# Differential attention scores: from twelve half-row matmuls a head to eight full-row ones

## The chip, the cores and the metric

The kernel runs on one core of one Trainium2 chip. The metric is the time of one execution on the device, in microseconds (us). A core has engines that run side by side, each with its own queue: TensorE multiplies matrices (PE in the profile, its weight loads are PEld), VectorE (DVE) and ScalarE (ACT) work element by element, GpSimd (POOL) does almost nothing here, and SyncE (SP) issues the transfers of the weights. An engine starts its instructions in the order of its queue; between engines there are semaphores.

A matmul takes a stationary operand (rows of the contraction by 128 columns), which a weight load puts into the array, and streams a moving operand through it. Its rows are the partitions of the on-chip memory: a contraction of 128 uses all 128 rows, one of 64 uses rows 0 to 63 or rows 64 to 127.

## The reference, cut to what matters

Two layers of an encoder with 256 tokens and 2048 features. In each layer a differential attention with 8 heads stands beside a latent attention with 8 heads; both are gated, summed and projected, and a feed-forward part and a gated embedding part follow. The part that the change touches:

```python
dq = apply_partial_rope(dq.reshape(b, s, 2 * DIFF_HEADS, DIFF_HEAD_DIM), cos_p, sin_p)
dk = apply_partial_rope(dk.reshape(b, s, 2 * DIFF_HEADS, DIFF_HEAD_DIM), cos_p, sin_p)
...
scores = jnp.einsum('bqhcd,bkhcd->bhcqk', qb, kh).astype(jnp.float32) * scale
probs = jax.nn.softmax(scores, axis=-1)
weights = probs[:, :, 0] - lam * probs[:, :, 1]
```

So each head has two attention maps (c = 0 and 1), each with its own 64 features of query and key, its own 256 x 256 scores and its own softmax; the second map is subtracted with a learned factor. All data are 32-bit floats.

## The kernel before, in words

**Numbers in two parts.** TensorE multiplies a shortened 32-bit format (float32r in the code). The kernel keeps precision by splitting each operand into two parts: the leading bits (hi), which ScalarE makes by a copy that rounds, and the rest (lo), which VectorE makes by subtracting hi from the number. A product a*b is then hi*hi + hi*lo + lo*hi. The function `split` (line 254) does this for activations, into a tile of 512 columns: hi of the 256 tokens, then their rest. The function `piece` (176) does it for weights: SyncE loads up to 128 x 1024 numbers, ScalarE writes `whi`, VectorE writes `wlo` (line 194; the subtraction is recorded at line 76, in the helper `tt`). `whi` and `wlo` have three buffers each. `emit` (216) issues, for each 128 x 128 block, one matmul of 512 columns with the hi weights (219) and one of 256 columns with the lo weights (223). `joined` (247) adds the two halves of the result: a ScalarE copy and a VectorE addition.

**The stage.** Activations are kept transposed: features on the partitions, tokens along the row. Within a layer, the differential heads come first. For a head h, `queries_keys(h)` (551) multiplies the layer's input with the query weights and then with the key weights of the head, 16 blocks each. Rows 0 to 63 of the result are map 0, rows 64 to 127 are map 1. Each result is joined, rotated (a shuffle of rows, two multiplications by the tables `sr` and `cr`, and an addition, all on VectorE) and split: the query into `ub[h]`, the key into the buffer `fa(h)`.

`diff_weights(h)` (662) computes the two score maps. The three products of the parts are listed by `three` (410), and `scores` (413) issues them for each block of 128 queries, the two maps in turn, so that a matmul on rows 64 to 127 and one on rows 0 to 63 alternate (line 421):

```python
def three(q, k):
    return [(q[:, :T], k[:, T:]), (q[:, T:], k[:, :T]), (q[:, :T], k[:, :T])]
```

That is 2 maps x 2 blocks x 3 products = 12 matmuls of 64 rows a head. `exps` (424) does the softmax of one map: the maximum of each row (VectorE, 427), a scaling of it, two exponentials with row sums (ScalarE, 430), a reciprocal (VectorE, 431). Then the two maps are combined into one matrix of weights E (669, 670), `turned` (434) transposes it on TensorE through `ident` (439) into a buffer with the tag `wt`, and `diff_out` (673) multiplies it with the values (679). Its result goes into `fa(h)`, by then free of the keys.

The latent attention's heads, later, use `scores` too, but with all 128 rows: ten matmuls of 256 columns a head. Its rotated queries are stored in another form, by the last branch of `rotated` (387 to 391): one ScalarE copy of 512 columns writes the rounded number twice, and two subtractions of 64 rows overwrite half of each copy with the rest, so that 128 rows hold the leading bits of 64 features and their rest.

**Order.** The loop `pipelined` (697) interleaves: it computes the scores of head h + 1 while the output of head h is made, and between these steps it takes one step of `beside` (604), which holds the products of later heads, the latent keys and queries, and the first gates. The program is written in that order, and a planner then orders the instructions of all engines by a timeline of its own: an instruction that can't start gives way to a later one that can. That is why scores of a head may stand in the middle of a later product. Buffers of one tag are handed on when their last reader is done; the planner inserts these waits.

Of the kernel before, what the change touches and what calls it, by code (L numbers as in the profile page):

```python
# [24 lines left out]
DH = 8  # L25
# [29 lines left out]
def encoder(ctx, tc, x, p, positions, cols, lams, wq, wk, wv, wcq, wckv, wkr, wga, wgb,  # L55
            w_q_up, w_kn, w_v, w_bd, w_bm, w_out, w_gate, w_up, w_down, w_pin, w_pg, rope_c, out):
    nc = tc.nc
    V, A, PE = nc.vector, nc.scalar, nc.tensor
# [4 lines left out]
    tmp = pool("tmp")  # L63
    stat = pool("stat")
# [4 lines left out]
    def scratch(tag, bufs, n=T):  # L69
        return tmp.tile([P, n], F32, tag=tag, name=tag, bufs=bufs)  # L70
# [4 lines left out]
    def tt(o, a, b, op):  # L75
        return V.tensor_tensor(out=o, in0=a, in1=b, op=op)  # L76

    def stt(o, a, s, b, op0, op1):
        return V.scalar_tensor_tensor(out=o, in0=a, scalar=s, in1=b, op0=op0, op1=op1)
# [40 lines left out]
    halves = rc[:, 4 : 4 + P]  # L120
# [28 lines left out]
    neg_lam = const.tile([P, DEPTH], F32, name="neg_lam")  # L149
# [97 lines left out]
    def joined(acc, o=None):  # L247
        t = scratch("join", 3)
        A.activation(t, acc[:, T:], AF.Copy)  # L249
        o = scratch("a", 4) if o is None else o  # L250
        tt(o, acc[:, :T], t, ALU.add)
        return o

    def split(u, src, gain=None):
        hi, lo = u[:, :T], u[:, T:]
        if gain is None:
            return A.activation(hi, src, AF.Copy), tt(lo, src, hi.bitcast(F32), ALU.subtract)  # L257
        return A.activation(hi, src, AF.Copy, scale=gain), stt(lo, src, gain, hi.bitcast(F32), ALU.mult, ALU.subtract)
# [108 lines left out]
    for t in krs:  # L367
        nc.gpsimd.memset(t.bitcast(F32), 0.0)

    def rotated(a, c_, s_, o=None):  # L370
        if o is None:
            r = bank()[:, :T]
            PE.matmul(r, halves, a, start=True, stop=True)
        else:
            r = a
        t = scratch("sh", 2)
        V.stream_shuffle(t, r, SWAP16)
        tt(t, t, s_, ALU.mult)
        tt(a, r, c_, ALU.mult)
        tt(a, a, t, ALU.add)  # L380
        if o is None:
            hi, rest = krs
            A.activation(hi[:, :T], a, AF.Copy)
            for j in range(2):
                s, t = slice(64 * j, 64 * j + 64), slice(j * T, (j + 1) * T)
                tt(rest[s, t], a[s], hi[s, :T].bitcast(F32), ALU.subtract)
        else:
            A.activation(o.rearrange("p (h t) -> p h t", h=2), a.rearrange("p (h t) -> p h t", h=1).to_broadcast([P, 2, T]), AF.Copy)
            for j in range(2):
                s, t = slice(64 * j, 64 * j + 64), slice(j * T, (j + 1) * T)  # L390
                tt(o[64 - 64 * j : 128 - 64 * j, t], a[s], o[s, t].bitcast(F32), ALU.subtract)

    def narrow(src, us):

# [15 lines left out]
    def three(q, k):  # L410
        return [(q[:, :T], k[:, T:]), (q[:, T:], k[:, :T]), (q[:, :T], k[:, :T])]

    def scores(*maps):


        Ss = [bank(ps_s, "S", "S", (P, 2, T)) for _ in maps]
        for b in range(2):
            for j in range(len(maps[0])):
                for S, pairs in reversed(list(zip(Ss, maps))):
                    q, k = pairs[j]  # L420
                    PE.matmul(S[:, b, :], q[:, b * P : (b + 1) * P], k, start=j == 0, stop=j == len(pairs) - 1)  # L421
        return Ss

    def exps(S, E, scale):

        nm, sm, rs = (stat.tile([P, 2], F32, tag=t, name=t, bufs=4) for t in ("nm", "sm", "rsum"))
        V.tensor_reduce(out=nm, in_=S, axis=AX.X, op=ALU.max, negate=True)
        ts(nm, nm, scale, None, ALU.mult)
        for b in range(2):
            last_exp[0] = A.activation(E[:, b, :], S[:, b, :], AF.Exp, bias=nm[:, b : b + 1], scale=scale, accum_out=sm[:, b : b + 1])  # L430
        V.reciprocal(out=rs, in_=sm)
        return rs
# [72 lines left out]
    for L in range(DEPTH):  # L505
# [38 lines left out]
        cr, sr, crm, srm = (t[:, j, :] for t in (fc(0), fc(1)) for j in range(2))  # L544
# [1 line left out]
            tt(o, t, R, ALU.mult)  # L546


        qk = [(ub[h], operand(fa(h, F32R))) for h in range(DH)]

        def queries_keys(h, *inside):
            for which, w in enumerate((wq, wk)):
                a = joined(product(w[L, h], ua, inside=(8, inside[which]) if inside else None))
                sh = scratch("sh", 2)
                V.stream_shuffle(sh, a, ROPE16)
                tt(sh, sh, sr, ALU.mult)
                tt(a, a, cr, ALU.mult)
                tt(a, a, sh, ALU.add)
                split(qk[h][which], a)


        cq, ckv = ub[8:12], ub[12:14]
# [99 lines left out]
        def diff_weights(h):  # L662
            q, k = qk[h]
            E = [weights(), weights("E1")]
            halves = [slice(c * 64, (c + 1) * 64) for c in range(2)]
            r = [exps(S, e, 0.125) for S, e in zip(scores(*(three(q[d], k[d]) for d in halves)), E)]
            ts(r[1], r[1], neg_lam[:, L : L + 1], None, ALU.mult)
            for b in range(2):
                A.activation(E[0][:, b, :], E[0][:, b, :], AF.Copy, scale=r[0][:, b : b + 1])
                stt(E[0][:, b, :], E[1][:, b, :], r[1][:, b : b + 1], E[0][:, b, :], ALU.mult, ALU.add)  # L670
            return E[0]

        def diff_out(h, W):
# [97 lines left out]
        for part, (f0, f1) in enumerate(FF_PARTS):  # L771
            for f in range(f0, f1):
                a = pre.pop(0) if pre else joined(product(w_gate[L, f], ub))
                tt(a, a, R, ALU.mult)
                s = scratch("sig", 2)
# [3 lines left out]
                b = pre.pop(0) if pre else joined(product(w_up[L, f], ub))  # L779
# [241 lines left out]
```

## Time and profile before

The profile is one execution, read by the hardware profiler.

| What | Value |
|---|---|
| time, median of 3 runs | 2827.17 us (2827.13 to 2827.33) |
| time of the profiled execution | 2827.12 us |
| its span, first to last instruction | 2825.3 us |
| TensorE busy | 2816.8 us, 100% |
| TensorE weight loads busy | 2490.3 us, 88% |
| VectorE busy | 2080.3 us, 74% |
| ScalarE busy | 1534.1 us, 54% |
| mean granted TensorE clock | 0.999 |
| bytes moved by DMA | 531.37 MB, mean 188 GB/s |

A row of a timeline gives the start, the duration, the engine, the line in the kernel, the instruction, what it writes and reads by the program's names, and the shapes (partitions x elements). Instructions on an engine overlap: the next one starts before the last one has ended. What an instruction costs in a full queue is therefore the distance from its start to the next start. In a row with "x12", twelve instructions of one kind are merged, and the duration reaches from the first start to the last end. The differential heads of the first layer lie at about 100 to 220 us of the span, those of the second at about 1504 to 1624 us.

### The profile page before, as it was taken

What the parts mean: (1) busy time and instruction counts of PE and PEld (TensorE: products, weight loads), DVE (VectorE), ACT (ScalarE), POOL (GpSimd) and SP (SyncE); (2) the same over time, 40 slices, a digit from 0 to 9 for tenths busy, and PEclk for the clock granted to TensorE, in tenths of its full rate; (3) what the DMA queues carried; (4) which work ended last, traced back from release to release, by engine and by line L of the source; (5) the groups of instructions that cost most, each with busy time, mean ns of one, the idle gap of its engine ahead of it and who ended that gap; (6) DMA issues with size and microseconds to landing.
All of it is one profiled execution on the core that took longest, in us unless ns stands there. A gap on an engine that the chain in (4) does not pass through costs nothing.

```text
span 2825.3 us, 43994 instructions
## 1 busy us (share of the span) xinstructions
PE 2816.8 (100%) x16691; PEld 2490.3 (88%) x16691; DVE 2080.3 (74%) x3573; ACT 1534.1 (54%) x2556; POOL 1.9 (0%) x15
## 2 busy tenths in 40 slices
PE   9999999999999999999999999999999999999998
PEld 8888988888888888888888889888888888888888
DVE  8998668776666666677869976687766666666777
ACT  7676546554444444455646765465544444444556
POOL 0000000000000000000000000000000000000000
PEclk9999999999999999999999999999999999999999
DMA  7545456555665566666665454555566655655654
GB/s 246 174 162 172 157 186 197 193 193 194 188 198 194 190 194 198 193 194 193 194 193 166 157 173 157 193 198 193 194 194 189 198 193 185 202 194 194 193 193 155
DMA packets 158325, 531.37 MB, mean 188 GB/s; under 512 B 17184, under 2 KB 25376, under 8 KB 158112
## 3 DMA queue, kind: packets, MB, share of 16 engines
q1 hardware_dynamic: 157680, 527.96, 58.2%
q8 instruction: 131, 2.15, 0.3%
q14 instruction: 82, 0.67, 0.1%
q10 hardware_dynamic: 432, 0.59, 0.1%
HBM read 526.39 MB, written 2.10 MB: 187 GB/s over the span
## 4 chain that ended last, share of the span: by engine, by line
PE 99%; DMA 0%; DVE 0%; SPq 0%; DVEq 0%; ACT 0%; issue 0%
PE mm L219 61%; PE mm L223 31%; PE S L421 1%; PE mmv L481 1%; PE mmv L483 1%; PE mmv L482 1%; PE at L439 1%; PE at L679 1%; PE at L735 0%; PE mm L826 0%; PE mm L407 0%; DMA w<-in_wv 0%; PE at L694 0%; PE at L332 0%; PE mm L882 0%; PE at L300 0%
## 5 line engine op out<-in xcount | busy, mean ns | idle before, releaser
L194 ACT ACTIVATE whi<-w 128x1024 fp32r<-128x1024 f32 (+2 forms) x1038 | 1065.9, 1028 | 1224.9 <-issue 593.4
L76 DVE TENSOR_TENSOR wlo<-w,whi 128x1024 fp32r<-128x1024 f32 (+2 forms) x1038 | 1225.8, 1182 | 648.0 <-ACT whi L194 642.3
L219 PE MATMUL mm<-ub,whi 128*128 128x512 f32 x3936 | 1340.5, 389 | 0.0
L219 PE MATMUL mm<-ua,whi 128*128 128x512 f32 x3712 | 1274.0, 390 | 0.0
L223 PE MATMUL mm<-ub,wlo 128*128 128x256 f32 x3936 | 1084.6, 276 | 0.0
L223 PE MATMUL mm<-ua,wlo 128*128 128x256 f32 x3712 | 1027.4, 277 | 0.0
L219 PEld LDWEIGHTS mm<-ub,whi 128*128 128x128 f32 x3936 | 737.8, 188 | 151.8
L219 PEld LDWEIGHTS mm<-ua,whi 128*128 128x128 f32 x3712 | 696.2, 188 | 141.5
L223 PEld LDWEIGHTS mm<-ub,wlo 128*128 128x128 f32 x3936 | 738.8, 188 | 1.3
L223 PEld LDWEIGHTS mm<-ua,wlo 128*128 128x128 f32 x3712 | 697.1, 188 | 2.0
L76 DVE TENSOR_TENSOR a<-mm,join 128x256 f32<-128x256 f32 (+1 forms) x423 | 174.8, 417 | 1.7 <-ACT join L855 1.4
L249 ACT ACTIVATE join<-mm 128x256 f32<-128x256 f32 x452 | 165.6, 368 | 6.3 <-PE mm L223 5.7
L76 DVE TENSOR_TENSOR xT<-xT,mm 128x256 f32<-128x256 f32 x256 | 106.9, 420 | 40.8 <-PE mm L223 37.0
L76 DVE TENSOR_TENSOR a<-a,row 128x256 f32<-128x256 f32 (+1 forms) x209 | 87.6, 422 | 5.9
L76 DVE TENSOR_TENSOR a<-a 128x256 f32<-128x256 f32 x120 | 50.9, 425 | 4.0
L76 DVE TENSOR_TENSOR ua<-a,ua 128x256 fp32r<-128x256 f32 x120 | 50.0, 418 | 1.0 <-ACT ua L257 1.0
L257 ACT ACTIVATE ua<-a 128x256 fp32r<-128x256 f32 x120 | 48.1, 403 | 2.6 <-DVE a L76 2.6
L481 PE MATMUL mmv<-whi,ua 128*128 128x512 f32 x128 | 49.0, 394 | 0.4 <-ACT whi L194 0.2
L430 ACT ACTIVATE E<-S,nm 128x256 f32<-128x256 f32 x96 | 44.2, 472 | 8.0 <-DVE nm L82 8.0
L482 PE MATMUL mmv<-whi,ua 128*128 128x512 f32 x128 | 48.4, 391 | 0.0
L483 PE MATMUL mmv<-wlo,ua 128*128 128x512 f32 x128 | 42.4, 392 | 0.0
L76 DVE TENSOR_TENSOR ssq<-ssq,sq 128x256 f32<-128x256 f32 x96 | 40.2, 419 | 0.3 <-ACT sq L287 0.3
(207 smaller groups left out, 1211.4 us busy)
## 6 DMA issues: line engine op xcount, KB each, us to landing
w<-in_w_gate SPq DMA_DIRECT2D x176, 512.0 KB, 4.6
w<-in_w_up SPq DMA_DIRECT2D x176, 512.0 KB, 4.7
w<-in_w_down SPq DMA_DIRECT2D x128, 512.0 KB, 4.2
w<-in_wga SPq DMA_DIRECT2D x64, 512.0 KB, 3.8
w<-in_wgb SPq DMA_DIRECT2D x64, 512.0 KB, 3.8
w<-in_w_out SPq DMA_DIRECT2D x64, 512.0 KB, 4.6
w<-in_w_pg SPq DMA_DIRECT2D x64, 512.0 KB, 4.6
w<-in_w_down SPq DMA_DIRECT2D x64, 384.0 KB, 3.7
```

The costliest lines, as they stand in the source:

```text
L76: return V.tensor_tensor(out=o, in0=a, in1=b, op=op)
L194: last_split[:] = A.activation(hi[:, s], w[:, s], AF.Copy), tt(lo[:, s], w[:, s], hi[:, s].bitcast(F32), ALU.subtract)
L219: lead = PE.matmul(acc, hi[:, s], u, start=start, stop=False)
L223: rest = PE.matmul(acc[:, T:], lo[:, s], u[:, :T], start=False, stop=stop)
L249: A.activation(t, acc[:, T:], AF.Copy)
L257: return A.activation(hi, src, AF.Copy), tt(lo, src, hi.bitcast(F32), ALU.subtract)
L421: PE.matmul(S[:, b, :], q[:, b * P : (b + 1) * P], k, start=j == 0, stop=j == len(pairs) - 1)
L430: last_exp[0] = A.activation(E[:, b, :], S[:, b, :], AF.Exp, bias=nm[:, b : b + 1], scale=scale, accum_out=sm[:, b : b + 1])
L439: PE.transpose(tp[:, kb, b * P : (b + 1) * P], W[:, b, kb * P : (kb + 1) * P], ident)
L481: PE.matmul(banks[k][b], xh, hi[:, s], start=c == 0, stop=False)
L482: PE.matmul(banks[k][b], xl, hi[:, s], start=False, stop=False)
L483: last_mm[:] = [PE.matmul(banks[k][b], xh, lo[:, s], start=False, stop=c == n - 1)]
```

## The change

**Queries.** `queries_keys` writes the joined query and key into the two halves of one tile of 2 x 256 columns (`qk`, with a second one, `qksh`, for the shuffled copy, both with the tag `wt`) and rotates both at once: one shuffle of 512 columns, two multiplications and one addition of 512 columns, with the tables read twice. The query is then stored in the stacked form that the latent queries have; that code becomes a function of its own, `stacked`. In columns 0 to 255, rows 0 to 63 hold the leading bits of map 0 and rows 64 to 127 its rest; in columns 256 to 511, rows 64 to 127 hold the leading bits of map 1 and rows 0 to 63 its rest.

**Keys.** Each map's key gets a tile of its own. Its 64 rows are split in place, by a ScalarE copy and a VectorE subtraction of 64 rows, and a further ScalarE copy puts the 512 columns (leading bits and rest) on the other 64 rows as well. The two tiles of a head are `fa(4)` and `fa(5)` for heads 1, 3 and 5, and `fa(6)` and `fa(7)` for the others.

**Scores.** A stacked query times a key's leading bits on all 128 rows gives (hi + rest) * hi in one matmul, and times the key's rest gives (hi + rest) * rest in another. A map takes two matmuls of 128 rows for each block of queries: 8 a head. The product of the two rests, left out before, is now included.

**Softmax.** The two maps of a head share one scaling of the maxima, one reciprocal and tiles of four columns.

```diff
+    def stacked(o, a):
+        A.activation(o.rearrange("p (h t) -> p h t", h=2), a.rearrange("p (h t) -> p h t", h=1).to_broadcast([P, 2, T]), AF.Copy)
+        for j in range(2):
+            s, t = slice(64 * j, 64 * j + 64), slice(j * T, (j + 1) * T)
+            tt(o[64 - 64 * j : 128 - 64 * j, t], a[s], o[s, t].bitcast(F32), ALU.subtract)
...
-        qk = [(ub[h], operand(fa(h, F32R))) for h in range(DH)]
+        qk = {}
+
+        def two(row):
+            return row.rearrange("p (h t) -> p h t", h=1).to_broadcast([P, 2, T])
 
         def queries_keys(h, *inside):
+            a, sh = (tmp.tile([P, 2, T], F32, tag="wt", name=n, bufs=4) for n in ("qk", "qksh"))
             for which, w in enumerate((wq, wk)):
-                a = joined(product(w[L, h], ua, inside=(8, inside[which]) if inside else None))
-                sh = scratch("sh", 2)
-                V.stream_shuffle(sh, a, ROPE16)
-                tt(sh, sh, sr, ALU.mult)
-                tt(a, a, cr, ALU.mult)
-                tt(a, a, sh, ALU.add)
-                split(qk[h][which], a)
+                joined(product(w[L, h], ua, inside=(8, inside[which]) if inside else None), a[:, which, :])
+            V.stream_shuffle(operand(sh), operand(a), ROPE16)
+            tt(sh, sh, two(sr), ALU.mult)
+            tt(a, a, two(cr), ALU.mult)
+            tt(a, a, sh, ALU.add)
+            q, k = a[:, 0, :], a[:, 1, :]
+            ks = [operand(fa(j + (4 if h in (1, 3, 5) else 6), F32R)) for j in range(2)]
+            qk[h] = ub[h], ks
+            stacked(ub[h], q)
+            for j in range(2):
+                s, t = slice(64 * j, 64 * j + 64), slice(64 - 64 * j, 128 - 64 * j)
+                split(ks[j][s], k[s])
+                A.activation(ks[j][t], ks[j][s].bitcast(F32), AF.Copy)
...
         def diff_weights(h):
             q, k = qk[h]
             E = [weights(), weights("E1")]
-            halves = [slice(c * 64, (c + 1) * 64) for c in range(2)]
-            r = [exps(S, e, 0.125) for S, e in zip(scores(*(three(q[d], k[d]) for d in halves)), E)]
-            ts(r[1], r[1], neg_lam[:, L : L + 1], None, ALU.mult)
+            qs = [q[:, d * T : (d + 1) * T] for d in range(2)]
+            Ss = scores(*([(a, b[:, T:]), (a, b[:, :T])] for a, b in zip(qs, k)))
+            nm, sm, r = (stat.tile([P, 4], F32, tag=t, name=t, bufs=2) for t in ("nm4", "sm4", "r4"))
+            for d, S in enumerate(Ss):
+                V.tensor_reduce(out=nm[:, 2 * d : 2 * d + 2], in_=S, axis=AX.X, op=ALU.max, negate=True)
+            ts(nm, nm, 0.125, None, ALU.mult)
+            for d, S in enumerate(Ss):
+                for b in range(2):
+                    j = 2 * d + b
+                    last_exp[0] = A.activation(E[d][:, b, :], S[:, b, :], AF.Exp, bias=nm[:, j : j + 1], scale=0.125, accum_out=sm[:, j : j + 1])
+            V.reciprocal(out=r, in_=sm)
+            ts(r[:, 2:], r[:, 2:], neg_lam[:, L : L + 1], None, ALU.mult)
...
```

More of the change, by code (lines that the diff above doesn't have):

```diff
@@ L387, in rotated @@
         else:
[L388 to L391, printed above, removed]
+            stacked(o, a)
     def narrow(src, us):
@@ L664, in diff_weights @@
             E = [weights(), weights("E1")]
-            halves = [slice(c * 64, (c + 1) * 64) for c in range(2)]
-            r = [exps(S, e, 0.125) for S, e in zip(scores(*(three(q[d], k[d]) for d in halves)), E)]
-            ts(r[1], r[1], neg_lam[:, L : L + 1], None, ALU.mult)
+            qs = [q[:, d * T : (d + 1) * T] for d in range(2)]
[10 more added lines that the diff above has]
+            ts(r[:, 2:], r[:, 2:], neg_lam[:, L : L + 1], None, ALU.mult)
             for b in range(2):
-                A.activation(E[0][:, b, :], E[0][:, b, :], AF.Copy, scale=r[0][:, b : b + 1])
-                stt(E[0][:, b, :], E[1][:, b, :], r[1][:, b : b + 1], E[0][:, b, :], ALU.mult, ALU.add)
+                A.activation(E[0][:, b, :], E[0][:, b, :], AF.Copy, scale=r[:, b : b + 1])
+                stt(E[0][:, b, :], E[1][:, b, :], r[:, 2 + b : 3 + b], E[0][:, b, :], ALU.mult, ALU.add)
             return E[0]
```

## The prediction

> **What bounds the kernel now.** I read the page from the top: the busy shares, then the chain that ended last.
>
> ```profile
> span 2825.3 us, 43994 instructions
> PE 2816.8 (100%) x16691; PEld 2490.3 (88%) x16691; DVE 2080.3 (74%) x3573; ACT 1534.1 (54%) x2556; POOL 1.9 (0%) x15
> PE 99%; DMA 0%; DVE 0%; SPq 0%; DVEq 0%; ACT 0%; issue 0%
> ```
>
> TensorE issues all the time and the chain is TensorE to 99%. So a microsecond taken from VectorE or ScalarE is worth nothing here, one taken from TensorE is worth itself, and one added to VectorE or ScalarE is worth nothing as long as the split weights still reach TensorE in time. A busy share over the whole span hides the stage that the change touches, so next I asked for the two stretches in which the eight differential heads of each layer run, and for the waits of the weight loads around the first.
>
> ```profile
> 100.00:220.00 120.00, 120.00 (x776) 105.10 (x775) 114.81 (x291) 89.93 (x226) 0.00 (x0) 1.00 0.49 161
> 1504.00:1624.00 120.00, 120.00 (x776) 105.14 (x775) 114.78 (x291) 90.33 (x226) 0.00 (x0) 1.00 0.50 161
> 110.00:130.00 20.00, 20.00 (x125) 17.45 (x124) 20.00 (x49) 15.16 (x34) 0.00 (x0) 1.00 0.59 189
> PEld S L421 <- issue: 1.2, 5, 0.2
> ```
>
> The columns are length, then busy time of PE, PEld, DVE, ACT, POOL, then the granted clock. In this stage VectorE has 114.81 of 120 us, so only 5.19 us are free, and between 110 and 130 us it has none. ScalarE has 30.07 us free. TensorE waits for no other engine; the only idle time of its loads is 0.2 us at the head of some score groups. That is the picture to keep: TensorE bounds, VectorE stands right behind it.
>
> **TensorE: the score matmuls.** Now a head has 12 half-row matmuls; afterwards 8 full-row ones. The durations in the page overlap, so a cost is read as the distance between starts. A head's group, with its neighbours, a second one that transposes follow, and the full-row scores of the latent attention:
>
> ```profile
> 106.48 0.28 PE L223 MATMUL mm<-ub,wlo 128*128 128x256 f32 x1
> 106.68 0.97 PE L421 MATMUL S<-fa,ub 64*128 64x256 f32 x12
> 107.58 0.50 PE L219 MATMUL mm<-ub,whi 128*128 128x512 f32 x1
> 107.92 0.28 PE L223 MATMUL mm<-ub,wlo 128*128 128x256 f32 x1
> ...
> 138.31 0.39 PE L219 MATMUL mm<-ua,whi 128*128 128x512 f32 x1
> 138.54 0.28 PE L223 MATMUL mm<-ua,wlo 128*128 128x256 f32 x1
> 138.74 0.97 PE L421 MATMUL S<-fa,ub 64*128 64x256 f32 x12
> ...
> 140.37 0.28 PE L223 MATMUL mm<-ua,wlo 128*128 128x256 f32 x1
> ...
> 322.83 0.28 PE L223 MATMUL mm<-ua,wlo 128*128 128x256 f32 x1
> 322.94 0.52 PE L421 MATMUL S<-fb,fa 128*128 128x256 f32 x3
> ...
> 324.14 0.60 PE L439 MATMUL at<-ident,E 128*128 128x128 f32 x4
> ...
> 324.81 0.28 PE L223 MATMUL mm<-ua,wlo 128*128 128x256 f32 x1
> ```
>
> Twelve half-row matmuls last 107.58 - 106.68 = 0.90 us. The group also starts late (0.20 us behind the low product of 106.48, where 322.94 follows 322.83 by 0.11) and the product behind it is late too (0.34 to its low part, where 138.31 to 138.54 takes 0.23). Ten full-row score matmuls take 324.14 - 322.94 = 1.20 us, 0.12 each, so eight take 0.96, and show no late start. First kind: 107.92 - 106.48 = 1.44 us becomes 0.11 + 0.96 + 0.23 = 1.30, a gain of 0.14. Second kind: 140.37 - 138.54 = 1.83; the latent one is 324.81 - 322.83 = 1.98 with ten, so 1.74 with eight, a gain of 0.09. Sixteen heads (eight, twice) gain 1.4 to 2.2 us; I take 1.8. At 0.11 per matmul (the step at 322.83) they would gain 16 x 8 x 0.01 = 1.3 us more, which is the far end: 3.1 us.
>
> A rule speaks against this part. The Trainium skill, "TensorE: Matmul & The Clock Gate", Part 3, says that matmuls on different row groups run concurrently and start about 4 ns apart. By it alone twelve half-row matmuls would cost six steps of 0.11 us, 0.66, against 0.96 for eight full-row ones: 0.30 us a head lost, 4.8 in all, where the rows above give 1.8 gained. What the rows can't exclude of it is a rival below. "TensorEngine Tiling (Array Packing)", Key Properties, says that a change of tiling mode drains the engine, and by that the late starts go with the half rows. The 0.20 against 0.11 us agrees.
>
> **VectorE per head.** Steps between starts, with a 512-column row and the only half-row pair that exists:
>
> ```profile
> 97.64 0.45 DVE L555 STREAM_SHUFFLE sh<-a 128x256 f32<-128x256 f32 x1
> 97.98 0.14 DVE L79 SCALAR_TENSOR_TENSOR ry<-ra,ry 128x2 f32<-128x2 f32 x1
> 98.12 0.43 DVE L76 TENSOR_TENSOR sh<-sh,fc 128x256 f32<-128x256 f32 x1
> 98.46 0.42 DVE L76 TENSOR_TENSOR a<-a,fc 128x256 f32<-128x256 f32 x1
> 98.80 1.22 DVE L76 TENSOR_TENSOR wlo<-w,whi 128x1024 fp32r<-128x1024 f32 x1
> ...
> 101.15 0.69 DVE L76 TENSOR_TENSOR wlo<-w,whi 128x512 fp32r<-128x512 f32 x1
> 101.76 0.42 DVE L76 TENSOR_TENSOR a<-mm,join 128x256 f32<-128x256 f32 x1
> ...
> 117.52 0.16 DVE L431 RECIPROCAL rsum<-sm 128x2 f32<-128x2 f32 x1
> 117.60 0.40 DVE L76 TENSOR_TENSOR a<-a,sh 128x256 f32<-128x256 f32 x1
> ...
> 213.41 0.85 DVE L76 TENSOR_TENSOR ub<-a,ub 64x256 fp32r<-64x256 f32 x2
> 214.29 0.17 DVE L431 RECIPROCAL rsum<-sm 128x2 f32<-128x2 f32 x1
> ```
>
> A 256-column operation steps 0.34 us, a 512-column one 0.61. The rotary of query and key together: six multiplies and adds become three, 2.04 to 1.83; two shuffles of 0.34 (97.64 to 97.98) become one, 0.68 to about 0.61 (no 512-column shuffle exists; the product's step is its nearest row). The softmax loses one small scaling and one reciprocal, about 0.08 each by the step 117.52 to 117.60: -0.16. The low parts were two full-row subtractions, 0.68; they are now four half-row ones. The pair at 213.41 takes 0.88, so four take 1.76: +1.08. Half the rows do not make an operation shorter. Sum: -0.21 - 0.07 - 0.16 + 1.08 = +0.64 us per head. If half-row ones cost 0.34 like full ones the sum is +0.24, the low end; a pause of 0.1 at each change of rows makes it +1.0. I take 0.8, since the new pairs change rows more often than the pair shown: 6.4 us a layer against 5.19 us free.
>
> **ScalarE per head.** Two roundings of 256 columns become one of 512 over both copies, two half-row ones, and two half-row copies of 512.
>
> ```profile
> 108.79 0.41 ACT L257 ACTIVATE ub<-a 128x256 fp32r<-128x256 f32 x1
> 109.10 0.37 ACT L249 ACTIVATE join<-mm 128x256 f32<-128x256 f32 x1
> ...
> 211.28 0.62 ACT L388 ACTIVATE ub<-a 128x512 fp32r<-128x512 f32 x1
> 211.80 0.47 ACT L430 ACTIVATE E<-S,nm 128x256 f32<-128x256 f32 x1
> ```
>
> 0.31 steps for 256 and 0.52 for 512 columns: from 0.62 to 0.52 + 0.62 + 1.04 = 2.18, +1.56 us per head, 12.5 us a layer in 30.07 us free. Copies that cross the halves are not shown; the nearest rows are the 0.52 above. I cost this at nothing because the free time covers it; without that cover it costs 25 us. Each copy waits for a subtraction on VectorE, and what is queued behind it is the next weight rounding (L194), on which VectorE's low part and then TensorE depend.
>
> **What is moved.** The query's rotary now waits for the key's product, one product later. Nobody on TensorE waits for it until the scores, and other products are placed in between; but four operations of 0.34 us (1.4 us) that were done early come after the key's join. The keys use four buffers by turns (4 and 5, or 6 and 7): head 7 writes those of head 6, whose scores come a step earlier, and the outputs of heads 4 and 5 take buffers that head 5's scores have left; no wait lands on TensorE. The four exponentials now wait for both maxima, and the transposes of E come a whole step later: nothing. No DMA is added, moved or removed.
>
> **Where VectorE's 0.8 us show.** What is late next is the low part of a weight piece. Its tightest places in the trace, a VectorE row and the first reader, counted at eight low products per 1024-column piece:
>
> ```profile
> 112.52 1.22 DVE L76 TENSOR_TENSOR wlo<-w,whi 128x1024 fp32r<-128x1024 f32 x1
> 114.57 0.28 PE L223 MATMUL mm<-ua,wlo 128*128 128x256 f32 x1
> 118.37 1.23 DVE L76 TENSOR_TENSOR wlo<-w,whi 128x1024 fp32r<-128x1024 f32 x1
> 121.50 0.28 PE L223 MATMUL mm<-ua,wlo 128*128 128x256 f32 x1
> ```
>
> The leads are 114.57 - (112.52 + 1.22) = 0.83 and 121.50 - (118.37 + 1.23) = 1.90 us. By 118 us heads 0 and 1 have brought 2 x 0.8 = 1.6 and the late rotary 1.4, together 3.0 against 1.90, in a stretch without free time: 1.1 us of TensorE waiting. Behind it six heads bring 4.8 us into some 5 free; I add 0.9 for what falls where none is free, between 0 (all fits) and 4.8 (none does). Two us a layer, 4 in all.
>
> Sum against the profiled execution, 2827.12 us (span 2825.3 and 1.8 around it; the median is 2827.17): 2827.1 - 1.8 + 4.0 = 2829.3 us, about 2829.
>
> **Rivals.**
> Nothing waits: the planner moves rotary work into free time. For: six of VectorE's 0.34 us steps merge, and typical pieces lead by more than those shown. Then 2827.1 - 1.8 = 2825.3 us; with the far end 2824.0.
> VectorE becomes the bound: none of the 0.8 us is hidden. For: 20.00 of 20.00 busy and 6.4 against 5.19 us. 16 x 0.8 - 1.8 = +11.0, so 2838 us. It decides the sign, with 5.65 us as 0.2%, when VectorE costs TensorE over (5.65 + 1.8) / 16 = 0.47 us a head.
> ScalarE is blocked: each of two copies waits for a low part that stands behind one weight piece (1.14 us, the step 98.80 plus 1.22 less the 0.08 of overlap). 1.56 + 2.3 = 3.9 us a head, as much as its 30.07 / 8 = 3.8 free; one such wait exposed a head gives 16 x 1.14 - 1.8 = +16.4, 2843.5 us. Against: pieces are rounded well ahead.
> The late starts stay: they belong to the scores, not to half rows. Six steps of 0.11 are 0.66 of the 0.90 + 0.09 + 0.11 = 1.10; the other 0.44 would stay beside 0.96, +0.30 a head, +4.8: 2831.9 us. This is where the packing rule named above ends. Against: the latent scores start 0.11 behind their neighbour.
>
> **How the numbers follow.** Some waiting, 2829: 0.45. Nothing waits: 0.19. VectorE bounds: 0.22. ScalarE blocked: 0.07. Late starts stay: 0.04. The rest, 0.03, is a gain over 0.2% from a cause I don't see: it would need 0.35 us a head, scores at 0.08 us a matmul. 0.2%, 5.65 us, is about what a measurement of this kernel can tell from no change. Faster 0.03, within 0.68, slower 0.29. The likeliest case alone spans 2826 to 2832; the range takes in the far end of the gain without waits, 2824, and half of the VectorE case, 2837.
>
> **What would show it.** Score groups of eight full-row matmuls, 0.96 us, starting 0.11 to 0.12 behind a low product. VectorE over 119 of the 120 us; half-row subtractions of 0.43 each, four a head; ScalarE near 102. New waits of PE or PEld for wlo near 114 to 122 and 1518 to 1526 us. No such rows means the second case; such rows in every head mean the third; PE waits for whi, with ScalarE idle before copies, the fourth. A wrong half-row price, or a planner that reorders the weight pieces, would make the prediction wrong.

## The result and the profile after

The changed kernel takes 2841.93 us (median of 6 runs, 2841.20 to 2843.36), the kernel before in the same rounds 2827.19 us (2826.92 to 2827.36). The ratio is 1.0053, 95% interval 1.0040 to 1.0066. So the change costs 14.7 us, 0.53%; 2829 was forecast, and the range ended at 2837.

From the page of the changed kernel, the span, the busy shares and the chain that ended last:

```profile
span 2840.5 us, 43839 instructions
...
PE 2821.6 (99%) x16627; PEld 2496.5 (88%) x16627; DVE 2089.5 (74%) x3493; ACT 1565.5 (55%) x2604; POOL 1.9 (0%) x15
...
PE 98%; DVE 1%; ACT 1%; issue 0%; DVEq 0%; ACTq 0%
```

From its windows, the two stretches with the differential heads (length, then busy time of PE, PEld, DVE, ACT and POOL, granted clock, DMA share, GB/s):

```profile
100.00:220.00 120.00, 115.11 (x697) 101.99 (x696) 109.91 (x231) 96.57 (x226) 0.00 (x0) 0.99 0.48 155
1504.00:1624.00 120.00, 114.94 (x689) 101.85 (x688) 107.43 (x224) 93.24 (x210) 0.00 (x0) 0.97 0.48 153
```

The page hardly moves: TensorE has gone from 100% to 99%, and the shares of the whole span would pass for no change at all. The windows tell it. TensorE had 120.00 of 120 us before and now stands idle for 4.89 and 5.06 us. VectorE is not fuller in these windows but emptier: 109.91 against 114.81 us. An engine that had become the bound of the stage would be busier; this one waits as well, though not where TensorE stalls (there it works 1.94 and 2.00 of 2 us, by rows further below). The granted clock, 1.00 before, is 0.99 and 0.97. The waits of TensorE over the whole span (total us, times, longest):

```profile
PE mm L219 <- DVE qk L76: 3.5, 2, 1.8
PE at L442 <- DVE E L79: 3.3, 2, 1.6
PE mm L219 <- DVE a L76: 3.2, 3, 1.5
```

Ten microseconds in six long waits and a short one, three long ones a layer, and none for a low part of the weights. "mm L219 <- DVE qk" and "<- DVE a" are products that wait until VectorE has joined an earlier result: a product needs one of the four PSUM banks of the pool `ps_mm`, and a bank comes free when the result in it has been joined. "at L442 <- DVE E" is the transposing of the weights E. TensorE's timeline of the changed kernel, first a score group, then the worst place of the first layer:

```profile
106.96 0.39 PE L219 MATMUL mm<-ua,whi 128*128 128x512 f32 x1
107.19 1.12 PE L424 MATMUL S<-fa,ub 128*128 128x256 f32 x8
108.14 0.28 PE L223 MATMUL mm<-ua,wlo 128*128 128x256 f32 x1
...
120.16 0.28 PE L223 MATMUL mm<-ub,wlo 128*128 128x256 f32 x1
122.09 0.94 PE L442 MATMUL at<-ident,E 128*128 128x128 f32 x4 [1.65 <-DVE E L79]
124.53 0.80 PE L219 MATMUL mm<-ua,whi 128*128 128x512 f32 x1 [1.50 <-DVE a L76]
```

The score group is as foreseen: eight matmuls in 108.14 - 107.19 = 0.95 us, 0.23 behind the 512-column product before them, which is a product's ordinary step. From 120.16 to 124.53 TensorE does little but four transposes, and then waits for a join. What VectorE did meanwhile:

```profile
103.69 0.87 DVE L76 TENSOR_TENSOR fa<-qk,fa 64x256 fp32r<-64x256 f32 x2
...
112.13 0.73 DVE L561 STREAM_SHUFFLE qksh<-qk 128x512 f32<-128x512 f32 x1
...
120.33 0.85 DVE L76 TENSOR_TENSOR ub<-qk,ub 64x256 fp32r<-64x256 f32 x2
121.22 0.42 DVE L76 TENSOR_TENSOR fa<-qk,fa 64x256 fp32r<-64x256 f32 x1
121.56 0.87 DVE L79 SCALAR_TENSOR_TENSOR E<-E,r,E 128x256 f32<-128x256 f32 x2
122.46 0.42 DVE L76 TENSOR_TENSOR fa<-qk,fa 64x256 fp32r<-64x256 f32 x1
122.91 1.23 DVE L76 TENSOR_TENSOR wlo<-w,whi 128x1024 fp32r<-128x1024 f32 x1
124.06 0.42 DVE L76 TENSOR_TENSOR a<-mm,join 128x256 f32<-128x256 f32 x1
124.39 0.74 DVE L76 TENSOR_TENSOR qk<-mm,join 128x256 f32<-128x256 f32 x2
```

The rotation of head 1 starts at 112.13; the last read of its joint tile `qk` ends at 122.46 + 0.42 = 122.88. Only then come the joins of head 2, query and key side by side ("x2" at 124.39). It looks as if they wait for head 1's tile, but the row of 103.69 speaks against it: it is the last read of head 0's joint tile and ends at 104.56, so a buffer of the tag `wt` had been out of use for 20 us. What the joins do wait for comes out of the experiments. Meanwhile the results of head 2's two products keep two of the four banks. The second layer has the same three long waits, of 1.5 to 1.8 us.

### The profile page after: what moved, and what is told of

The parts are those of the page before. It is cut to its first block, busy times and chain, and to the rows that moved or that the text cites. A ratio compares the mean times of both kernels' runs of the same rounds, so it can differ in the third digit from the quotient of the medians.

```text
span 2840.5 us, 43839 instructions
## 1 busy us (share of the span) xinstructions
PE 2821.6 (99%) x16627; PEld 2496.5 (88%) x16627; DVE 2089.5 (74%) x3493; ACT 1565.5 (55%) x2604; POOL 1.9 (0%) x15
## 4 chain that ended last, share of the span: by engine, by line
PE 98%; DVE 1%; ACT 1%; issue 0%; DVEq 0%; ACTq 0%
PE mm L219 60%; PE mm L223 30%; PE mmv L484 1%; PE mmv L486 1%; PE mmv L485 1%; PE S L424 1%; DVE wlo L76 1%; PE at L701 0%; PE at L442 0%; PE at L757 0%; PE mm L848 0%; PE mm L410 0%; ACT E L687 0%; DVE qk L76 0%; ACT whi L194 0%
## 5 line engine op out<-in xcount | busy, mean ns | idle before, releaser
L219 PE MATMUL mm<-ub,whi 128*128 128x512 f32 x3936 | 1340.4, 389 | 0.0
L219 PE MATMUL mm<-ua,whi 128*128 128x512 f32 x3712 | 1278.6, 391 | 6.7 <-DVE qk L76 3.5
L219 PEld LDWEIGHTS mm<-ub,whi 128*128 128x128 f32 x3936 | 737.7, 188 | 151.7
L219 PEld LDWEIGHTS mm<-ua,whi 128*128 128x128 f32 x3712 | 698.5, 188 | 150.8 <-ACT E L687 4.1
L76 DVE TENSOR_TENSOR a<-mm,join 128x256 f32<-128x256 f32 x391 | 162.0, 417 | 1.6 <-ACT join L877 1.4
L76 DVE TENSOR_TENSOR a<-a,sig 128x256 f32<-128x256 f32 x92 | 38.4, 419 | 0.0
```

The costliest lines, as they stand in the source:

```text
L219: lead = PE.matmul(acc, hi[:, s], u, start=start, stop=False)
```

## The experiments

The kernel before ran beside each group of runs: its medians were 2827.18 to 2827.35 us. "Window" is the stretch from 100 to 220 us in the first layer.

### The transposes held back

Does TensorE lose its time because the planner puts E's transposes too early? Here they are kept behind the next head's scores.

```diff
-            wt = turned(W)
+            with tc.issue_after(last_score[0].ins):
+                wt = turned(W)
```

> The changed kernel with one edit: the transposes of a head's weights may be issued on TensorE only after the scores of the next head, as they stood before the change for the first heads. No operation is added or removed. Theory 'order': TensorE lost its time because the planner put these transposes one product earlier in TensorE's queue, where E was not ready; then the waits near 120 to 125 us and 1530 to 1535 us go, with the clock drop behind them, about 10 of the 15 us: 2831 us or less. Theory 'VectorE': VectorE has too much work in this stage (the half-row subtractions), so TensorE waits the same time somewhere else: 2839 to 2842 us.

Measured: 2845.85 us (2844.18 to 2848.03), ratio 1.0066 (1.0051 to 1.0081), 3.9 us more than the changed kernel. TensorE's largest wait:

```profile
PE mm L219 <- DVE a L76: 12.0, 4, 4.1
```

The copy of head 0's transposed weights into a `wt` buffer, and the joins of head 2:

```profile
132.28 0.60 ACT L444 ACTIVATE wt<-at 128x512 f32<-128x512 f32 x1 [0.80 <-PE at L442]
...
133.85 0.75 DVE L76 TENSOR_TENSOR qk<-mm,join 128x256 f32<-128x256 f32 x2
```

The wait for E is gone, and the waits for a join have grown to 12 us. So the early transposes did not make the hole; held back, they make it larger. And the joins of head 2 went with them: in the changed kernel the copy starts at 124.74 and the joins at 124.39, here at 132.28 and 133.85.

### The softmax taken apart

```diff
-            nm, sm, r = (stat.tile([P, 4], F32, tag=t, name=t, bufs=2) for t in ("nm4", "sm4", "r4"))
...
+            r = [exps(S, e, 0.125) for S, e in zip(Ss, E)]
```

> The changed kernel with the softmax of each map by itself again, as before the change (two scalings and two reciprocals a head more than in the changed kernel). Theory 'merged softmax': four exponentials behind both maxima delay E and hold ScalarE; undone, the transposes of head 0 find E earlier and the time falls below 2835 us. Theory 'order': the transposes still stand ahead of the next product, so no large gain, 2838 to 2843 us. Theory 'VectorE': 0.16 us a head more on VectorE, 2842 to 2845 us.

Measured: 2841.16 us (2840.26 to 2841.76), ratio 1.0049 (1.0032 to 1.0065): 0.8 us less than the changed kernel, with overlapping ranges. (The edit adds one scaling and one reciprocal a head, not two of each; the 0.16 us is for one of each.) The common maxima and reciprocals cost next to nothing, as the prediction had it.

### The rotation taken apart

Query and key are joined and rotated one by one in `a` and `sh`, as before; scores, key copies and softmax stay changed.

```diff
-            a, sh = (tmp.tile([P, 2, T], F32, tag="wt", name=n, bufs=4) for n in ("qk", "qksh"))
...
+                a = joined(product(w[L, h], ua, inside=(8, inside[which]) if inside else None))
+                sh = scratch("sh", 2)
...
+                if which == 0:
+                    stacked(ub[h], a)
```

> The changed kernel with query and key rotated each by itself again, the query at once after its own product; the stacked query, the key copies, the full-row scores and the merged softmax stay. VectorE has 0.28 us a head more than in the changed kernel. Theory 'late rotary': the four query operations that came behind the key's product made the shortage near 118 us; undone, below 2833 us. Theory 'VectorE' by sum of work alone: 16 x 0.28 = 4 us more, 2842 to 2846 us. Theory 'order': it depends on where the transposes land; they stand one product later here, so about 2831 us.

Measured: 2828.49 us (2828.10 to 2829.09), ratio 1.0004 (0.9995 to 1.0014). This one edit gives back 13.4 of the 14.7 us. Its waits for VectorE in the two stages:

```profile
PE mm L223 <- DVE wlo L76: 1.4, 4, 0.4
```

Its window:

```profile
100.00:220.00 120.00, 119.24 (x737) 106.02 (x736) 115.89 (x278) 101.72 (x235) 0.00 (x0) 1.00 0.50 161
```

From VectorE's timeline, the join at the place of the worst wait:

```profile
118.23 0.42 DVE L76 TENSOR_TENSOR a<-mm,join 128x256 f32<-128x256 f32 x1
```

The join stands alone at 118.23, 6.2 us ahead of the pair at 124.39. What waits are left are for `wlo`, the mechanism that the prediction had priced. With the stall gone, VectorE and ScalarE do their work in the window, 115.89 and 101.72 us: their low figures in the changed kernel were an effect of the stall.

### The key copies on GpSimd

Is ScalarE blocked by the added copies?

```diff
-                A.activation(ks[j][t], ks[j][s].bitcast(F32), AF.Copy)
+                nc.gpsimd.tensor_copy(ks[j][t], ks[j][s].bitcast(F32))
```

> The changed kernel with the key copies to the other rows on GpSimd instead of ScalarE: ScalarE loses two copies of 0.64 us a head and the waits for VectorE in front of them. Theory 'ScalarE blocked': the copies hold up the weight roundings; without them below 2833 us. Theory 'VectorE': VectorE's work is unchanged, 2838 to 2843 us, or more if GpSimd slows VectorE. Theory 'order': the transposes of head 0 stand behind the next scores here, about 2831 us.

Measured: 2844.93 us (2843.47 to 2845.20), ratio 1.0061 (1.0046 to 1.0076). Its window:

```profile
100.00:220.00 120.00, 113.71 (x686) 100.69 (x684) 112.79 (x229) 88.95 (x211) 16.36 (x16) 0.97 0.46 148
```

Its largest wait:

```profile
PE mm L219 <- DVE a L76: 8.7, 2, 4.3
```

ScalarE is busy for 7.6 us less than in the changed kernel and nothing is won. But GpSimd takes 16.36 / 16 = 1.0 us a copy, longer than ScalarE, so this run alone does not clear ScalarE. The run with the rotations apart does: there ScalarE makes all the copies, with 101.72 us of work in the window, and the stall is gone.

### Whose buffers: the joint tile out of the shared tag

The rotation together differs from the one apart in two things: it comes later, and its tiles `qk` and `qksh` share the tag `wt`, four buffers, with the transposed weights. Two heads' joint tiles fill all four. Here `qk` lies in two tiles, by turns, that back `ub[14]` and `ub[15]`, unused in this stage; `qksh` and the transposed weights stay.

```diff
-            a, sh = (tmp.tile([P, 2, T], F32, tag="wt", name=n, bufs=4) for n in ("qk", "qksh"))
+            a = ux(14 + h % 2, F32)
+            sh = tmp.tile([P, 2, T], F32, tag="wt", name="qksh", bufs=4)
```

> The changed kernel, all of it, with one difference: the joint tile of query and key (qk) lies in two tiles of the list ub that are unused in this stage, by turns, instead of in the four buffers with the tag wt, which it shared with its shuffled copy and with the transposed weights. No operation is added or removed. Theory 'buffer': the join of a head's query and key waits for one of four wt buffers, so the products' PSUM banks stay full and TensorE waits for a bank; with other buffers the waits of several us go, and 2826 to 2831 us is left, like the run with rotations apart. Theory 'late rotary': rotating the query only behind the key's product bunches VectorE's work whatever the buffer; 2838 to 2843 us.

Measured: 2834.28 us (2833.33 to 2836.13), ratio 1.0025 (1.0016 to 1.0035), 7.6 us less than the changed kernel. Its waits for VectorE in the heads' stages:

```profile
PE at L724 <- DVE ub L79: 4.9, 2, 2.5
...
PE mm L227 <- DVE wlo L76: 0.7, 2, 0.4
```

From VectorE's timeline, the join of head 2's query:

```profile
118.34 0.41 DVE L76 TENSOR_TENSOR ux<-mm,join 128x256 f32<-128x256 f32 x1
```

The joins of query and key are apart again, at 118.34 and 125.29, and all waits for a bank and for E are gone. A new wait of 2.5 us a layer stands at the end of the stage (near 231 and 1639 us), where transposes wait for work that VectorE has put off.

### The counterpart: the transposed weights out of the tag

Here `qk` and `qksh` keep the four buffers to themselves, and the transposed weights of heads 0 to 5 take the two unused tiles.

```diff
-            wt = turned(W)
+            wt = turned(W, o=ux(14 + h % 2, F32) if h < 6 else None)
```

> The changed kernel, all of it, but the transposed weights of heads 0 to 5 lie in two unused tiles of the list ub, by turns; query, key and shuffled copy have the four wt buffers to themselves. It is the counterpart of the run in which the joint tile was moved. Theory 'buffer': the waits near 120 and 142 us of both layers go as they did there, 2826 to 2835 us. If it was the joint tile's place in ub that helped and not the number of buffers: 2839 to 2843 us.

Measured: 2831.08 us (2830.71 to 2831.75), ratio 1.0014 (1.0004 to 1.0024), 10.9 us less than the changed kernel. Its waits for VectorE in the stages:

```profile
PE mm L223 <- DVE a L76: 1.6, 2, 0.8
...
PE mm L227 <- DVE wlo L76: 0.7, 2, 0.4
```

From VectorE's timeline, the join:

```profile
118.15 0.42 DVE L76 TENSOR_TENSOR qk<-mm,join 128x256 f32<-128x256 f32 x1
```

The rotations are together as in the changed kernel, and the work is the same. Whichever of the two users leaves the tag, the join comes 6 us earlier and the long waits near 120 and 142 us go. So the shared tag is the cause of most of the loss. How it acts is inferred, since no row names a buffer that VectorE waits for: the planner had already put the join later in VectorE's queue. The transposed weights of head h stand ahead of the joint tile of head h + 2 in the program. In the changed kernel, the copies of heads 0 and 1 and the joins of head 3 (those of head 2 start at 124.39):

```profile
124.74 0.57 ACT L444 ACTIVATE wt<-at 128x512 f32<-128x512 f32 x1
...
143.05 0.75 DVE L76 TENSOR_TENSOR qk<-mm,join 128x256 f32<-128x256 f32 x2
...
143.82 0.61 ACT L444 ACTIVATE wt<-at 128x512 f32<-128x512 f32 x1
```

The join of the query of head h + 2 stands beside the copy of head h, within 1.4 us for all six such pairs of the first layer. In the run above that held the transposes back the joins went back too; here, with the weights out of the tag, they come long before the copies: 118.15 against 127.16, and 131.49 against 147.05. All this fits a tag that hands out its buffers in the order of the program, so that a joint tile gets none before the transposed weights ahead of it have theirs, whether or not one is free. A lack of buffers does not fit, as the row of 103.69 showed. The run with `qk` moved out has the same lock on the shuffled copy, which stayed in the tag: head 3's key is joined at 139.37, and its shuffle comes at 148.40, behind the copy at 146.52.

### The key split over all rows

The added VectorE work by itself: the key is split once over 128 rows (one rounding, one subtraction), and three half-row ScalarE copies make the two tiles. That takes away both half-row subtractions of the key, but not those of the query.

```diff
-            for j in range(2):
-                s, t = slice(64 * j, 64 * j + 64), slice(64 - 64 * j, 128 - 64 * j)
-                split(ks[j][s], k[s])
-                A.activation(ks[j][t], ks[j][s].bitcast(F32), AF.Copy)
+            split(ks[0], k)
+            A.activation(ks[1][64:], ks[0][64:].bitcast(F32), AF.Copy)
+            A.activation(ks[1][:64], ks[0][64:].bitcast(F32), AF.Copy)
+            A.activation(ks[0][64:], ks[0][:64].bitcast(F32), AF.Copy)
```

In the changed kernel:

> The changed kernel with one difference: the key is split once over all 128 rows and put into place by three half-row copies on ScalarE; rotations together, wt buffers shared. VectorE has about 0.5 us a head less than in the changed kernel. Theory 'buffer': the waits near 120 us stay, since the joint tile still waits for a wt buffer; 2836 to 2842 us. Theory 'VectorE': the half-row subtractions caused the loss, and with two of the four gone most of it goes; below 2832 us.

Measured: 2840.88 us (2840.09 to 2841.71), ratio 1.0049 (1.0034 to 1.0064). Its largest wait:

```profile
PE at L442 <- DVE E L79: 7.3, 2, 3.7
```

Less work for VectorE (107.03 us in the window) leaves the stall, now as a wait for E: 1.0 us less than the changed kernel, with overlapping ranges. In the kernel with the rotations apart:

> The changed kernel with rotations apart, and the key split once over all 128 rows (one rounding, one subtraction) and then put into place by three half-row copies of 512 columns on ScalarE, where the change has two half-row splits and two copies. VectorE loses one half-row subtraction and its change of rows, about 0.5 us a head; ScalarE gains about 0.3. Theory 'VectorE' for what is left over the kernel before (1.2 us with rotations apart): the waits for wlo shrink, 2826 to 2828 us. If ScalarE now holds up the weight roundings: over 2829 us.

Measured: 2825.74 us (2825.11 to 2825.89), ratio 0.9994 (0.9984 to 1.0003). The window:

```profile
100.00:220.00 120.00, 120.00 (x745) 107.54 (x744) 115.48 (x274) 103.50 (x236) 0.00 (x0) 1.00 0.51 165
```

TensorE has 120.00 of 120 us again, and no wait of it lies in the stage. This is the change without both its losses, 2.75 us under the version with half-row splits of the key. With more rounds:

> The version with rotations apart and the key split once over all rows, again, in five rounds: it had no wait left on TensorE in this stage, and by the prediction's own arithmetic for the scores (1.4 to 2.2 us gained) it should lie 1.4 to 2.2 us below the kernel before, 2825.0 to 2825.8 us, with an interval that tells whether the gain is real. If the scores gain nothing: 2827 us.

Measured: 2825.71 us (2825.46 to 2825.98), ratio 0.9995 (0.9986 to 1.0004). All 11 runs lie below all runs of before (2826.68 to 2827.84); the interval of the ratio still holds 1. It is the best version found, 1.5 us under the kernel before.

### Both remedies, with the rotations together

The two diffs above together, in the changed kernel:

```diff
+            a = ux(14 + h % 2, F32)
...
+            split(ks[0], k)
```

> The changed kernel with both remedies and the rotations still together: the joint tile in ub, the key split once over all rows with three copies. VectorE has the least work of all these versions. If buffer and half-row subtractions are the two causes, no wait is left and the gain of the full-row scores shows: 2825 to 2827 us, at or below the version with rotations apart and the same key split. If rotating late costs by itself, 2829 us or more.

Measured: 2829.22 us (2828.45 to 2829.60), ratio 1.0007 (0.9998 to 1.0016). Its largest wait for VectorE in the stages:

```profile
PE mm L223 <- DVE a L76: 2.4, 2, 1.2
```

Its window:

```profile
100.00:220.00 120.00, 119.67 (x737) 106.80 (x736) 109.51 (x227) 98.09 (x220) 0.00 (x0) 1.00 0.51 162
```

3.5 us remain above the version with the rotations apart, though VectorE has 6 us less in the window (109.51 against 115.48; over the whole span 2082.4 against 2084.4, so most of the 6 is only put off). So the sum of VectorE's work does not decide; when it comes does. The sharing is not quite gone here, since `qksh` is still in the tag. Head 3's key is joined at 139.15, and its shuffle comes only beside the copy of head 1's transposed weights:

```profile
146.22 0.74 DVE L566 STREAM_SHUFFLE qksh<-ux 128x512 f32<-128x512 f32 x1
...
146.76 0.59 ACT L448 ACTIVATE wt<-at 128x512 f32<-128x512 f32 x1
```

So the 3.5 us are not the price of the late rotation alone.

### Parts of the change in the kernel before

Its two splits made in half rows, nothing else changed:

```diff
-                split(qk[h][which], a)
+                for s in (slice(0, 64), slice(64, 128)):
+                    split(qk[h][which][s], a[s])
```

> The kernel before with the splits of query and key in two half-row instructions each: ScalarE four roundings of 64 rows instead of two of 128, VectorE four subtractions of 64 rows instead of two of 128, nothing else. It measures what the half-row subtractions cost by themselves. By the prediction's price VectorE gets about 1.08 us a head, 8.6 us a layer, against 5.19 us free: some waiting, 2829 to 2835 us. If half rows are free in practice because the planner finds room: 2827 us.

Measured: 2828.88 us (2828.42 to 2829.20), ratio 1.0005 (0.9996 to 1.0014). The window:

```profile
100.00:220.00 120.00, 120.00 (x770) 104.78 (x770) 118.54 (x303) 95.90 (x235) 0.00 (x0) 1.00 0.50 159
```

VectorE rises from 114.81 to 118.54 of 120 us, and 1.5 us is all that comes of it: an engine at 99% of a stage need not bound it.

The joint rotation in the kernel before, in the `wt` buffers, and then with the joint tile in the unused tiles:

```diff
+            a, sh = (tmp.tile([P, 2, T], F32, tag="wt", name=n, bufs=4) for n in ("qk", "qksh"))
...
-                split(qk[h][which], a)
+            for which in range(2):
+                split(qk[h][which], a[:, which, :])
```

> The kernel before with one part of the change alone: query and key of a head are joined into one tile of the wt buffers and rotated together, then split as before; half-row scores, no stacked query, no key copies, softmax as before. VectorE has 0.28 us a head less than before. Theory 'buffer' (and 'late rotary'): TensorE waits for PSUM banks as in the changed kernel, 2833 to 2842 us. Theory 'VectorE' by sum of work: no loss, 2825 to 2828 us.

```diff
+            a = ux(14 + h % 2, F32)
+            sh = tmp.tile([P, 2, T], F32, tag="wt", name="qksh", bufs=4)
```

> The kernel before with the rotations of a head's query and key together, as in the earlier run of that kind, but the joint tile in the two unused tiles of ub instead of the shared wt buffers. Nothing else of the change. Against the version in the wt buffers (2830.2 us): theory 'buffer' says the wt buffers made that loss too, so 2827 us or, with 0.28 us a head less on VectorE, a little below. Theory 'late rotary' says that rotating the query only behind the key's product costs by itself: 2829 to 2831 us.

Measured: 2830.22 us (2829.94 to 2830.48), ratio 1.0009 (1.0000 to 1.0019), and 2828.74 us (2828.19 to 2829.42), ratio 1.0005 (0.9996 to 1.0014). The largest wait of the first for VectorE in the stages; the second has none there:

```profile
PE mm L219 <- DVE a L76: 1.4, 2, 0.7
```

Alone, the joint rotation costs 2.9 us, and about half of that goes with the joint tile out of the tag. The same rotation costs 13.4 us beside the other parts of the change, though in the first of these runs the joins keep to the copies as well (head 2's at 126.08 behind 123.22, head 3's at 138.14 behind 137.48). Why it costs so much more beside the other parts was not shown.

## Why the prediction was wrong

Step by step from the kernel before: 2827.2, less 1.5 for the full-row scores (the rotations apart and the key split over all rows, 2825.7); plus 2.75 for the key's half-row splits (2828.5); plus 13.4 for the rotations together in the shared tag (2841.9). Of these, 10.9 go when the transposed weights leave the tag (2831.1); 2.6 stay.

- **"What is moved" failed.** It said "no wait lands on TensorE". It followed the buffers of the keys, `fa(4)` to `fa(7)`, one by one, and the products in between, and passed over the tag on the added line: `qk` and `qksh` take `wt`, which has four buffers and another user. The query's join is not only "one product later"; it comes only when the transposed weights of two heads before have got their buffer, the results of both products stay in two of the four banks, and TensorE runs out of banks. This is 10.9 of the 13.4 us. That the sharing costs this is shown by the two runs that take one of its users out of the tag; that the order of the program decides, and not the number of buffers, is inferred from their rows. So what stands ahead of the prediction, that a buffer is handed on when its last reader is done, is not all: it also has to be the next one's turn.
- **"What is late next is the low part of a weight piece" was wrong** for the changed kernel, where a join and E were late. It was right for the kernel with the rotations apart, whose only waits for VectorE are for `wlo`.
- **The VectorE term was the right mechanism and a little too large.** Two half-row subtractions step 121.22 - 120.33 = 0.89 us, against the 0.88 used. Over the whole span VectorE's busy time grew by 2089.5 - 2080.3 = 9.2 us, 0.58 a head, against 0.64 in the sum and 0.8 taken. The term was 4.0 us; the key's half rows measured 2.75 with changed scores, and half-row splits of query and key in the kernel before 1.5.
- **The scores were right**: 0.95 against 0.96 us a group, no late start, and a gain of 1.5 where 1.4 to 2.2 was the range (a net gain, in a version with what else is left of the change). The rival with late starts falls. So does the loss of 4.8 us that the prediction worked out from the packing rule of the Trainium skill, "TensorE: Matmul & The Clock Gate", Part 3, taken alone: by it this version would have been slower than before.
- **ScalarE's copies lie beside other work**, as foreseen. Two of them take 1.28 us:

```profile
123.56 1.28 ACT L572 ACTIVATE fa<-fa 64x512 fp32r<-64x512 f32 x2
```

That is 0.64 each against the 0.52 taken. "ScalarE near 102" holds where nothing stalls (101.72). "VectorE over 119" holds neither there (115.89) nor in the changed kernel (109.91).
- **The rival "VectorE becomes the bound" came near the number, 2838, by a mechanism that did not happen.** In the changed kernel's stage VectorE is less busy than before, and with work taken from it the time was 1.0 us less, within overlapping ranges. That the number was near is luck.
- **A part of the loss had no term at all**: the clock behind the waits (below).

Open: why the rotations together still cost 2.6 us with the transposed weights out of the tag (2831.08 against 2828.49). The later rotation and the order that the planner makes of it were not told apart. The 1.5 us in the kernel before and the 3.5 us beside the other remedies come from versions in which the shuffled copy still shares the tag. No run has the key split over all rows, the rotations together, and nothing shared.

## What to carry to other kernels

When a change takes scratch tiles from an existing tag, list every user of that tag in the order of the program, and ask of each tile what the one ahead of it waits for; counting the buffers is not enough. Here, by this reading, a join that had to wait its turn kept its PSUM bank, and so stopped TensorE, which never touches that buffer. Two operations joined into one save issue time on their engine, but the first result waits for the second, and its memory is held for that long. When TensorE idles while the engine it waits for has become emptier too, look for memory that is handed on late before you look for work to take away.

## What the runs showed of the hardware

The waits cost more than their length. Windows of 2 us of the changed kernel, around the first two long waits of the first layer, its third, the first two of the second and its third (the last three columns are granted clock, DMA share and GB/s):

```profile
122.00:124.00 2.00, 0.87 (x4) 0.45 (x4) 1.94 (x4) 1.98 (x5) 0.00 (x0) 1.00 0.24 83
124.00:126.00 2.00, 1.47 (x5) 1.29 (x6) 2.00 (x5) 1.95 (x5) 0.00 (x0) 0.62 0.29 94
126.00:128.00 2.00, 2.00 (x8) 1.71 (x8) 2.00 (x6) 0.44 (x2) 0.00 (x0) 0.52 0.64 215
...
142.00:144.00 2.00, 0.38 (x2) 0.37 (x3) 1.83 (x4) 1.99 (x9) 0.00 (x0) 1.00 0.36 119
144.00:146.00 2.00, 2.00 (x14) 1.76 (x13) 2.00 (x6) 2.00 (x5) 0.00 (x0) 1.00 0.69 225
...
1534.00:1536.00 2.00, 1.51 (x5) 1.32 (x6) 2.00 (x5) 1.95 (x5) 0.00 (x0) 0.55 0.36 113
1536.00:1538.00 2.00, 2.00 (x9) 1.68 (x9) 2.00 (x6) 0.42 (x1) 0.00 (x0) 0.60 0.64 209
...
1552.00:1554.00 2.00, 0.41 (x2) 0.40 (x3) 2.00 (x4) 2.00 (x9) 0.00 (x0) 1.00 0.32 109
1554.00:1556.00 2.00, 2.00 (x11) 1.73 (x10) 2.00 (x6) 2.00 (x5) 0.00 (x0) 0.67 0.73 225
1556.00:1558.00 2.00, 2.00 (x8) 1.71 (x8) 2.00 (x5) 0.78 (x3) 0.00 (x0) 0.50 0.12 45
```

Behind three of these four places the granted clock falls to about a half: 8 matmuls in 2 us, where 14 is usual. By an estimate from these rows the drops cost 2 x (0.38 + 0.48), 2 x (0.45 + 0.40) and 2 x (0.33 + 0.50) us, each 1.7 us, which is 3.4 us at half clock. That is some 5 us beside the 10 us of the waits, together about 15 of the 15.2 by which the span grew (the scores' 1.5 us of gain leave as much unexplained). The waits near 142 and 1552 us are alike, 1.7 and 1.8 us, and only the second brought a drop. It would also explain why the changed kernel's runs spread over 2.2 us and those of the kernel before over 0.4; that is argued.

The Trainium skill, "TensorE: Matmul & The Clock Gate", Part 1, has the clock halved after an idle activity window of about 3.4 us, a window that runs on by itself. The length of the drops agrees, and so does it that like waits need not have like effects. The table of the same page of the Trainium skill, in "Why this matters for your kernels", allows pauses of up to about 3 us; here a single wait of 1.8 us, in 2 us with 0.41 of work, was enough, so the measurement differs.
